# The low halves of the two gated branches computed on VectorE instead of GpSimd

## The chip, the cores and the metric

The kernel runs on one core of a Trainium2 chip. A core has five engines that run side by side, each with its own in-order instruction queue: TensorE (PE: matmuls, with PEld for its weight loads), VectorE (DVE), ScalarE (ACT), GpSimd (POOL) and SyncE (SP, which here only issues DMAs). They wait for one another through semaphores. The metric is device time in microseconds (us) of one execution, over several runs. A profile is one more execution under the hardware profiler.

## The reference

Two layers of a transformer trunk for 512 latent and 256 context tokens, model width 1024. Each layer has two parallel attention branches that share one input projection: A is a 2-D neighbourhood attention with 8 heads of 64 channels, B is a grouped-query attention with 8 query heads. Each branch is multiplied by its own gate, projected to the model width, weighted by a sigmoid gate, and the sum goes through one output projection:

```
def _merge(a_att, b_att, a_z, b_z, g_a, g_b, w_o_a, w_o_b, w_out):
    o_a = (a_att * jax.nn.silu(a_z)) @ w_o_a
    o_b = (b_att * jax.nn.silu(b_z)) @ w_o_b
    merged = jax.nn.sigmoid(g_a) * o_a + jax.nn.sigmoid(g_b) * o_b
    return merged @ w_out
```

The first factor of each product in front of `w_o_a` and `w_o_b` is what this document calls a gated branch. Layer 0 computes all 768 tokens, layer 1 only the 512 latent ones.

## The kernel before

Matmuls run in a reduced 32-bit format. To keep the accuracy, each operand is split into a high part (the value rounded to that format, a cast on ACT) and a low part (the value minus its high part, a subtraction), and a product is three matmuls: high by high, low by high, high by low. In the projections these are lines L433, L434 and L435 (`mm3`). For the first piece of branch B in layer 0 they are L458, L459 and L461, where the last is the one that reads the low part of the activations.

Weights are streamed from memory by SP into three rotating buffers (`raw`), cast on ACT to `whi` (L418 or L403) and subtracted to `wlo` (L420 or L406) on POOL or DVE in turn (`mix_lo`). The gated branches are split by `hilo`: for each of the four 128-channel groups f of a branch, ACT casts the whole token range (L656) and an engine that the caller chooses subtracts (L657). The names in the profile are `za` to `gah` and `gal` for branch A, and `zb` to `gbh` and `gbl` for branch B.

A layer goes through these stages: the input projections; the neighbourhood attention, head by head, in which the gate projections run as filling work for PE; the key, value and query projections of branch B; then the grouped-query attention, again head by head, with the rest of the gate projections and the whole of branch A's output projection (`o_chunks("a")`) as filling work; and last the merge, with branch B's output projection and `w_out`.

In the grouped-query stage each head has four tiles of 128 queries. Per tile PE makes the scores (L861, L862, into `pss`, of which there are two buffers), DVE takes the maximum and copies the scores (L1131), ACT takes the exponential (L1132) and casts (L802), DVE or POOL subtracts the low half (L803), and SP issues a transposing DMA (L804). The next tile's scores can be written when ACT has read the buffer. In layer 0 a context tile follows (L874, L876, L880). The values are L1148 and L1149. The row sums are inverted on DVE (L809), transposed on PE (L811) and multiplied into the gate on DVE (L812). A head ends with ACT L795, DVE L796 and a product L797 into `zb`.

`prepare` is the first piece of filling work of branch A's output projection: it splits all four groups of `za` and loads the sigmoid gates `tg` (L660, SP). Each piece of that projection has twelve matmuls into the only `psf` buffer, and DVE then multiplies the result into `tg` (L692), which frees the buffer. `early` runs before the values of the last head: it loads the other two `tg` and splits groups 0 to 2 of `zb`, which are complete by then. Group 3 is split at the start of the merge, on DVE in both kernels.

The order in which each engine runs its instructions is not that of the source. The tile framework places all engines' instructions with a planner that has its own model of their durations (`schedule_with_timeline_sim=True`), so that another engine for one instruction can move the others too. On the chip each engine then keeps that fixed order.

Of the kernel before, what the change touches and what calls it, by code (L numbers as in the profile page):

```python
# [50 lines left out]
def R(ap):  # L51
    return ap.bitcast(F32R)
# [18 lines left out]
def hybrid_kernel(es: ExitStack, tc, x, ctx, cvec, w_ada, w_ada0, small, gvec, w_in, w_o_a, w_o_b, w_out,  # L71
                  bias_int, bias_edge, rope, ident_d, out):
    nc = tc.nc
    V, S, G, T = nc.vector, nc.scalar, nc.gpsimd, nc.tensor
# [14 lines left out]
    def big(name):  # L89
        return bigp.tile([128, 3072], F32, tag="big", name=nm(name))  # L90
# [493 lines left out]
    def layer(l, hx, nxt, start):  # L584
# [62 lines left out]
        gated = {}  # L647

        def hilo_tiles(name):
            return [big(name + part).rearrange("p (f n) -> p f n", f=4) for part in "hl"]  # L650

        def hilo(src, dst, fs, lo_eng=G, parts=((0, ntok),)):
            sv = src.rearrange("p (f n) -> p f n", f=4)
            for n0, n1 in parts:
                for f in fs:
                    S.copy(R(dst[0][:, f, n0:n1]), sv[:, f, n0:n1])  # L656
                    lo_eng.tensor_tensor(R(dst[1][:, f, n0:n1]), sv[:, f, n0:n1], dst[0][:, f, n0:n1], ALU.subtract)  # L657

        def load_tg(c):
            nc.sync.dma_start(tg[c].rearrange("p (f n) -> p f n", f=4)[:, :, :ntok], gs[c][:, :, :ntok])  # L660

        def o_chunks(br, prepare, evac):

            src = (w_o_a if br == "a" else w_o_b)[l]
            act = lambda part, k: gated[br][part][:, k, :]
            res = []
            for i in range(4):
                st = {}

                def ld(i=i, st=st):  # L670
                    st["w"] = load_w2(src, 256 * i, 4, pool_lo if br == "b" and i == 0 else mix_lo)
                pieces = [lambda f=f, n0=n0, n1=n1, i=i, st=st:
                          chan_proj(st["w"], f, act, n0, n1, lambda f, a, b, ps: evac(2 * i + f, a, b, ps),
                                    3 if br == "b" and i == 0 and first else 0)
                          for f in range(2) for n0, n1 in spans]
                res.append((ld, ([prepare] if i == 0 and prepare else []) + pieces))
            return res

        def prepare():

            gated["a"] = hilo_tiles("ga")
            hilo(za, gated["a"], range(4))
            for c in (0, 2):
                tg[c] = big("tg")
                load_tg(c)
# [56 lines left out]
        za = big("za")  # L742
# [16 lines left out]
        if True:  # L759
# [329 lines left out]
            hp["lag"] = 2  # L1089
            qbv = big("qb").rearrange("p (j n) -> p j n", j=4)  # L1090
            fill = in_order(gates[n_na:] + o_chunks("a", prepare, evac_a))
            run(fill, 2)

# [15 lines left out]
            zb = big("zb")  # L1109
# [55 lines left out]
            def early():  # L1165

                for c in (1, 3):
                    tg[c] = big("tg")
                    load_tg(c)
                gated["b"] = hilo_tiles("gb")  # L1170
                hilo(zb, gated["b"], range(3))
            own = {"cb": vbig[:, 1152:2176].rearrange("p (v n) -> p v n", v=2),
                   "junk": vbig[:, 2176:2432].bitcast(BF16)}
            bg = gate_steps((1,), Parts(att["p"], own)) if first else []
            pipeline(fill, 8, gq_first, values_of(zb, gq_values, vs[:, 1:2]), early, bg)
            gq_es.close()

# [322 lines left out]
```

## Time and profile before

| | us |
|---|---|
| median of 3 runs | 1125.91 |
| lowest and highest | 1125.44 and 1126.06 |
| the profiled execution's own time | 1127.56 |
| its span, from first to last instruction | 1125.6 |
| PE busy | 1093.3 (97%) |
| DVE busy | 774.7 (69%) |
| ACT busy | 579.0 (51%) |
| POOL busy | 490.6 (44%) |

The profiled execution is 1.65 us above the median of the runs, and 1.96 us of it lie outside the span. All times of day below count from the start of the span. A busy PE is not PE at its peak: its clock is granted in steps, and at a lower clock the same matmuls are busy for longer.

### The profile page before, as it was taken

To read this page: it belongs to the slowest core of one execution; us is meant where nothing else is said; L and a number is where in the kernel's file an instruction comes from. 1 tells how busy PE (TensorE), PEld (TensorE's weight loads), DVE (VectorE), ACT (ScalarE), POOL (GpSimd) and SP (SyncE) were. 2 spreads that over 40 slices of the span, in tenths; PEclk is the share of its full clock that TensorE was granted. 3 is DMA by queue.
4 is the path that set the end of the run, shared out by engine and by line. 5 is a ranking of instruction groups with operands and counts; after the bars stand their busy time and mean duration, and the time that the engine had idled before them with its cause. 6 is when DMAs were issued, how large, how long until landed. Compare 5 with 4: busy or idle time off the path is not lost.

```text
span 1125.6 us, 16862 instructions
## 1 busy us (share of the span) xinstructions
PE 1093.3 (97%) x5826; PEld 905.3 (80%) x5826; DVE 774.7 (69%) x1492; ACT 579.0 (51%) x1154; POOL 490.6 (44%) x405
## 2 busy tenths in 40 slices
PE   8999999999999999979999999999999999999998
PEld 5688888888998877757788888888888987776677
DVE  4666788897466477776577785458878765677473
ACT  6453266665433576755330284326666446776431
POOL 1054254654247144454521545235554563563531
PEclk9999999999999999989999999999999999999999
DMA  9454322242351488869633532553333236989742
GB/s 373 143 172 140 114 63 66 73 136 89 93 168 38 123 201 185 185 172 269 173 108 125 183 129 72 142 174 92 100 107 116 59 105 172 188 224 239 197 145 80
DMA packets 192222, 161.29 MB, mean 143 GB/s; under 512 B 116364, under 2 KB 158088, under 8 KB 190472
## 3 DMA queue, kind: packets, MB, share of 16 engines
q1 hardware_dynamic: 184800, 145.82, 46.8%
q0 software_dynamic: 2368, 7.87, 2.1%
q10 hardware_dynamic: 4968, 6.53, 1.7%
q8 instruction: 46, 0.75, 0.3%
q14 instruction: 40, 0.33, 0.1%
HBM read 115.58 MB, written 17.32 MB: 118 GB/s over the span
## 4 chain that ended last, share of the span: by engine, by line
PE 38%; issue 4%; DVE 3%; DMA 3%; POOL 2%; ACT 1%; SPq 1%; POOLq 0%; ACTq 0%
PE psx L435 6%; PE psx L433 6%; PE psx L434 6%; PE psf L433 4%; PE psf L434 4%; PE psf L435 4%; PE pss L955 1%; PE pss L861 1%; POOL wlo L406 1%; PE pss L862 1%; PE pst L779 1%; PE pst L1148 1%; DMA raw<-in_w_o_a_dram 1%; PE pst L1149 1%; DMA raw<-in_w_in_dram 1%
## 5 line engine op out<-in xcount | busy, mean ns | idle before, releaser
L420 POOL TENSOR_TENSOR wlo<-raw,whi 128x512 fp32r<-128x512 f32 x70 | 97.9, 1405 | 106.1 <-ACT whi L418 70.4
L433 PE MATMUL psf<-hx,whi 128*128 128x512 f32 (+1 forms) x360 | 138.0, 383 | 3.2 <-ACT zt L614 2.4
L435 PE MATMUL psf<-hx,wlo 128*128 128x512 f32 (+1 forms) x360 | 135.8, 377 | 0.0
L434 PE MATMUL psf<-hx,whi 128*128 128x512 f32 (+1 forms) x360 | 135.1, 375 | 0.0
L433 PE MATMUL psx<-whi,hx 128*128 128x512 f32 (+1 forms) x328 | 120.8, 372 | 0.0
L434 PE MATMUL psx<-wlo,hx 128*128 128x512 f32 (+1 forms) x328 | 119.6, 366 | 0.0
L435 PE MATMUL psx<-whi,hx 128*128 128x512 f32 (+1 forms) x328 | 119.5, 365 | 0.0
L418 ACT CAST whi<-raw 128x512 fp32r<-128x512 f32 x136 | 82.3, 620 | 64.0 <-DMA raw<-in_w_in_dram 35.3
L406 POOL TENSOR_TENSOR wlo<-raw,whi 128x512 fp32r<-128x512 f32 x40 | 61.2, 1535 | 122.1 <-ACT whi L403 80.1
L803 POOL TENSOR_TENSOR h<-p,h 128x768 f16<-128x768 f32 (+1 forms) x40 | 65.7, 1644 | 96.4 <-ACT h L802 72.0
L403 ACT CAST whi<-raw 128x512 fp32r<-128x512 f32 x88 | 54.1, 623 | 99.2 <-PE psx L435 34.2
L420 DVE TENSOR_TENSOR wlo<-raw,whi 128x512 fp32r<-128x512 f32 x66 | 73.6, 1115 | 30.6 <-ACT whi L418 29.0
L504 POOL TENSOR_TENSOR ss<-ss,ehalf 128x8 f32<-128x8 f32 (+2 forms) x40 | 62.5, 1566 | 72.9 <-DVE ss L501 72.8
L433 PEld LDWEIGHTS psf<-hx,whi 128*128 128x128 f32 x360 | 67.9, 188 | 15.4 <-ACT zt L614 3.7
L435 PEld LDWEIGHTS psf<-hx,wlo 128*128 128x128 f32 x360 | 67.8, 188 | 11.6
L1131 DVE CUSTOM_DVE_ANT_0 p<-pss,vb 128x768 f32<-128x768 f32 x64 | 60.3, 953 | 23.6 <-PE pss L862 21.1
L434 PEld LDWEIGHTS psf<-hx,whi 128*128 128x128 f32 x360 | 67.9, 189 | 10.3
L1132 ACT ACTIVATE p<-pss,mx 128x768 f32<-128x768 f32 x64 | 57.6, 900 | 34.7 <-DVE mx L1131 33.7
L435 PEld LDWEIGHTS psx<-whi,hx 128*128 128x128 f32 x328 | 61.9, 189 | 10.0
L434 PEld LDWEIGHTS psx<-wlo,hx 128*128 128x128 f32 x328 | 62.0, 189 | 9.2
L433 PEld LDWEIGHTS psx<-whi,hx 128*128 128x128 f32 x328 | 61.8, 189 | 8.9
L435 PE MATMUL psx<-hx,wlo 128*128 128x256 f32 (+1 forms) x208 | 68.0, 327 | 0.0
(362 smaller groups left out, 3095.8 us busy)
## 6 DMA issues: line engine op xcount, KB each, us to landing
raw<-in_w_in_dram SPq DMA_DIRECT2D x168, 256.0 KB, 2.9
rawb<-in_w_ada_dram SPq DMA_DIRECT2D x48, 256.0 KB, 2.8
raw<-in_w_out_dram SPq DMA_DIRECT2D x32, 256.0 KB, 2.9
tg<-gs SPq DMA_DIRECT2D x4, 1536.0 KB, 6.8
rawx<-in_w_ada_dram SPq DMA_DIRECT2D x4, 1024.0 KB, 9.8
rawy<-in_w_ada_dram SPq DMA_DIRECT2D x4, 1024.0 KB, 9.5
gs<-zt ACTq DMA_DIRECT2D x16, 256.0 KB, 2.0
raw<-in_w_o_a_dram SPq DMA_DIRECT2D x16, 256.0 KB, 3.4
```

The lines of the kernel that those rows point to most:

```text
L403: S.copy(hi[:, :n], raw[:, :n])
L406: e.tensor_tensor(lo[:, :n], raw[:, :n], F(hi[:, :n]), ALU.subtract)
L418: S.copy(hi, raw)
L420: lo_eng(i).tensor_tensor(lo, raw, F(hi), ALU.subtract)
L433: T.matmul(ps, lhs[0], rhs[0], start=first, stop=False)
L434: T.matmul(ps, lhs[0], rhs[1], start=False, stop=False)
L435: T.matmul(ps, lhs[1], rhs[0], start=False, stop=last)
L504: G.tensor_tensor(ss, ss, ehalf[:, :n], ALU.pow)
L779: T.transpose(pt[:, c0:c0 + 128], src, ident)
L803: eng.tensor_tensor(h[:, 1], p[:, :n], h[:, 0], ALU.subtract)
L1131: V.tensor_tensor_reduce(p, pss, lift, -1.0, 3e38, ALU.add, ALU.min, mx[:, 0:1])
L1132: S.activation(p, pss, AF.Exp, bias=mx[:, 0:1], accum_out=r[:, i:i + 1])
```

## The change

The two calls of `hilo` that took GpSimd, its default, now pass VectorE: four subtractions (L657) for `gal` and three for `gbl` in each layer, of 128x768 elements in layer 0 and 128x512 in layer 1. What is computed is the same, and the casts (L656) stay on ACT.

```
         def prepare():
 
             gated["a"] = hilo_tiles("ga")
-            hilo(za, gated["a"], range(4))
+            hilo(za, gated["a"], range(4), V)
             for c in (0, 2):
                 tg[c] = big("tg")
                 load_tg(c)
...
                 gated["b"] = hilo_tiles("gb")
-                hilo(zb, gated["b"], range(3))
+                hilo(zb, gated["b"], range(3), V)
```

Since the planner places the instructions anew, the built order of the changed kernel differs from the point where `gal` is made in layer 0 on to the first part of layer 1, and in a few places later in layer 1. Up to the first `gal` the order of every engine is the same in both kernels.

More of the change, by code (lines that the diff above doesn't have):

```diff
@@ L681, in prepare @@
             gated["a"] = hilo_tiles("ga")
-            hilo(za, gated["a"], range(4))
+            hilo(za, gated["a"], range(4), V)
             for c in (0, 2):
@@ L1170, in early @@
                 gated["b"] = hilo_tiles("gb")
-                hilo(zb, gated["b"], range(3))
+                hilo(zb, gated["b"], range(3), V)
             own = {"cb": vbig[:, 1152:2176].rearrange("p (v n) -> p v n", v=2),
```

## Prediction

> **What bounds the kernel now.** I read the page's totals first, then busy time by stretch, PE's waits by who ended them, and the engines' instructions in order of time where PE stands still.
>
> ```profile
> span 1125.6 us, 16862 instructions
> PE 1093.3 (97%) x5826; PEld 905.3 (80%) x5826; DVE 774.7 (69%) x1492; ACT 579.0 (51%) x1154; POOL 490.6 (44%) x405
> ...
> 490.00:500.00 10.00, 4.13 (x15) 2.80 (x13) 9.94 (x5) 6.71 (x15) 9.91 (x7) 0.83 0.99 341
> 500.00:510.00 10.00, 7.85 (x29) 5.58 (x30) 6.46 (x11) 1.83 (x3) 3.49 (x3) 0.66 0.48 104
> ...
> 550.00:560.00 10.00, 9.70 (x57) 8.34 (x57) 6.70 (x7) 1.40 (x3) 8.82 (x7) 1.00 0.67 213
> ```
>
> PE is busy 97% of the span, so the kernel is bound by PE and all that a change can give is the remaining 32 us of gaps, plus time lost at a lowered clock. One place stands out: from 490 to 510 (columns: stretch, length, busy time of PE, PEld, DVE, ACT, POOL, then granted clock, DMA share, GB/s) PE works 11.98 of 20 us and the granted clock is 0.83 and 0.66. There the layer-0 `gal` is made.
>
> ```profile
> PE psv L811 <- DVE ho L796: 5.8, 1, 5.8
> ...
> PE psf L434 <- POOL gbl L657: 1.0, 1, 1.0
> PE psf L434 <- POOL gal L657: 0.6, 1, 0.6
> ```
>
> These are PE's waits that touch the change (total, times, longest). The longest of the kernel, 5.8 us, is for DVE's L796, not for L657 itself. The order of time shows why (columns: start, duration, engine, line):
>
> ```profile
> 487.45 1.66 POOL L803 TENSOR_TENSOR h<-p,h 128x768 f16<-128x768 f32 x1 [5.72 <-ACT h L802]
> 489.08 1.29 POOL L797 TENSOR_TENSOR zb<-zb,ho 64x512 f32<-64x512 f32 x1
> 490.32 1.27 POOL L420 TENSOR_TENSOR wlo<-raw,whi 128x512 fp32r<-128x512 f32 x1
> 491.54 7.15 POOL L657 TENSOR_TENSOR gal<-za,gah 128x768 fp32r<-128x768 f32 x4
> 498.63 1.29 POOL L420 TENSOR_TENSOR wlo<-raw,whi 128x512 fp32r<-128x512 f32 x1
> ...
> 490.42 0.96 DVE L1131 CUSTOM_DVE_ANT_0 p<-pss,vb 128x768 f32<-128x768 f32 x1
> ...
> 492.20 8.26 DVE L420 TENSOR_TENSOR wlo<-raw,whi 128x512 fp32r<-128x512 f32 x1
> 500.49 0.95 DVE L855 TENSOR_TENSOR qs<-qb,qs 64x768 fp32r<-64x768 f32 x1
> ...
> 501.67 0.42 DVE L796 TENSOR_TENSOR ho<-psv,ho 64x256 f32<-64x256 f32 x1
> ...
> 510.81 0.69 DVE L420 TENSOR_TENSOR wlo<-raw,whi 128x512 fp32r<-128x512 f32 x1 [1.94 <-ACT whi L418]
> ```
>
> An L420 on DVE takes 0.69 us at 510.81 and 8.26 us at 492.20. The long one ends at 500.46, 0.54 us after the last of POOL's five gapless instructions (498.63 + 1.29 = 499.92): DVE was kept from its operands while POOL ran `gal` and the next `wlo`. Behind it stood L855, L809, L796, on which PE's L811 waited, and all score passes.
>
> **The change, part by part.** POOL loses 14 instructions, in these groups (count, total us and mean ns):
>
> ```profile
> L657 POOL TENSOR_TENSOR gal<-za,gah 128x768 fp32r<-128x768 f32 x4 | 7.1, 1832 | 0.0
> L657 POOL TENSOR_TENSOR gbl<-zb,gbh 128x768 fp32r<-128x768 f32 x3 | 6.8, 2298 | 0.0
> L657 POOL TENSOR_TENSOR gal<-za,gah 128x512 fp32r<-128x512 f32 x4 | 5.6, 1452 | 0.5 <-ACT gah L656 0.5
> L657 POOL TENSOR_TENSOR gbl<-zb,gbh 128x512 fp32r<-128x512 f32 x3 | 3.8, 1281 | 0.0
> ...
> 485.17 0.96 DVE L803 TENSOR_TENSOR h<-p,h 128x768 f16<-128x768 f32 x1 [0.67 <-ACT h L802]
> ```
>
> POOL gives up 7.1 + 6.8 + 5.6 + 3.8 = 23.3 us. DVE gets seven of 128x768 at 0.96 us, the L803 of that size at 485.17, and seven of 128x512 at 0.69: 11.6 us, which lifts it from 774.7 to 786 us, 70% of the span. No DMA and no cast is added; the two `tg` loads and `prepare` keep their place.
>
> *Layer 0, branch A.* PE's rows there:
>
> ```profile
> 487.80 3.03 ACT L656 CAST gah<-za 128x768 fp32r<-128x768 f32 x4
> ...
> 491.90 0.39 ACT L614 ACTIVATE zt<-psf 128x256 f32<-128x256 f32 x1
> ...
> 492.33 0.49 PE L433 MATMUL psf<-gah,whi 128*128 128x512 f32 x1 [1.62 <-ACT zt L614]
> 493.42 0.80 PE L434 MATMUL psf<-gal,whi 128*128 128x512 f32 x1 [0.59 <-POOL gal L657]
> ...
> 502.15 0.69 PE L811 MATMUL psv<-ident,r 128*128 128x128 f32 x2 [5.80 <-DVE ho L796]
> ...
> 503.91 0.63 PE L434 MATMUL psf<-gal,whi 128*128 128x512 f32 x1
> 504.34 0.63 PE L435 MATMUL psf<-gah,wlo 128*128 128x512 f32 x1
> ...
> 505.95 0.90 ACT L1132 ACTIVATE p<-pss,mx 128x768 f32<-128x768 f32 x1 [9.12 <-DVE mx L1131]
> ...
> 512.77 0.50 PE L433 MATMUL psf<-gah,whi 128*128 128x512 f32 x1 [0.28 <-DVE tg L692]
> ...
> 541.47 0.40 PE L434 MATMUL psf<-gal,whi 128*128 128x512 f32 x1
> 541.71 0.40 PE L435 MATMUL psf<-gah,wlo 128*128 128x512 f32 x1
> ...
> 544.79 0.38 PE L1148 MATMUL pst<-ht,vb 128*128 128x512 f16 x1 [0.61 <-DMA ht<-h]
> ...
> 547.16 0.38 PE L1149 MATMUL pst<-ht,vb 128*128 128x512 f16 x1
> ```
>
> A 128x512 matmul follows the one before it after 0.24 us at full clock (541.47 to 541.71) and after 0.43 us in the slow stretch (503.91 to 504.34); half the columns take half. The twelve passes of a head's values start 0.22 us apart (544.79 to 547.16). I walk through the changed kernel's built order with these durations, with 0.7 and 0.45 us for 512- and 256-wide operations on DVE that have no row of their own here. Until 492.33 nothing can differ for PE: it waits for ACT's L614 as now. Casts of `gah` finish from 488.6 to 490.83. DVE's queue reads: `gal` 0, L874, `gal` 1 and 2, L876, L812, `gal` 3, L420, L1131, L855, L796, L809, L692, L1131, L803, L812, L692. POOL's run L803, L797, L420 (487.45 to 491.59) still contends; with one POOL instruction let past ahead of each of the first three `gal` they end at about 490.1, 492.3 and 494.5, `gal` 3 after L812 at 496.6, L420 at 497.3 and the first score pass L1131 at 498.2 (490.42 + 0.96 = 491.4 now). So this tile's softmax is 6.8 us *later* than now; that is the cost of the edit here. PE runs all twelve matmuls of the first `w_o_a` piece ahead of the second tile's scores and ends them at 497.3, just behind `gal` 3. Scores of tile 2: 498.0 (two of 512 and two of 256 columns, 0.7 us). Tile 3 needs the buffer of tile 1, released by its exponential (0.90) at 499.2, and ends at 499.9; L811 at 500.3 (L855, L796 and 0.2 us of L809 after 498.2). The second piece waits for L692 (0.7) to free `psf`: 500.5 to 501.9. Tile 4 waits for the exponential of tile 2 at 502.4, and ends at 503.1. The third piece waits for L692 behind an L803 and an L812, 503.3 to 506.1. Values take 2.6 us, the context values 0.6 (four half-width passes and their start) and the context scores 0.5: 509.8.
>
> In the trace of before the third piece starts at 512.77 and so ends at 512.77 + 12 x 0.23 = 515.5, with the same work behind it except the context values of 0.6 us: 516.1. **Gain 6.3 us**, if PE's clock is full. If it is low until 506.5 as now, each of the passages above that isn't waiting for DVE stretches by 0.43/0.23 and the walk ends 2.1 us later: gain 4.2 us. I take the middle, 5.2.
>
> The rule in the Trainium skill that bears on this speaks against the change: "SBUF — State Buffer", section "Who interferes with whom", has a VectorE instruction with two SBUF inputs and a GpSimd instruction that reads SBUF exclude each other, the later one waiting until the earlier one finishes. By it the moved subtractions meet the lock-out themselves, as the walk counts with rows of its own. The trace agrees with one instruction's wait at 550.79, quoted below, but at 492.20 the wait spanned five; by the page the lock-out alone would not explain that row, and the sum would be that of the second rival.
>
> *Layer 0, branch B.*
>
> ```profile
> 550.79 2.23 DVE L420 TENSOR_TENSOR wlo<-raw,whi 128x512 fp32r<-128x512 f32 x1
> ...
> 1002.62 1.44 DVE L420 TENSOR_TENSOR wlo<-raw,whi 128x512 fp32r<-128x512 f32 x1
> ...
> 1052.24 0.50 PE L434 MATMUL psf<-gbl,whi 128*128 128x512 f32 x1 [1.05 <-POOL gbl L657]
> ...
> 1081.17 7.74 POOL L406 TENSOR_TENSOR wlo<-raw,whi 128x512 fp32r<-128x512 f32 x2 [4.81 <-ACT whi L403]
> ```
>
> Here the POOL run of `gbl` holds DVE for only one instruction (2.23 us). Moved, three times 0.96 us stand in DVE's queue ahead of an L692 that frees `psf`; PE's built order has the b-branch's high parts to do meanwhile, and needs `gbl` 2 some 0.5 us after it gets there. PE waits about that long there now for L692 and the rest: I take 0. Without that cover the price is 3 x 0.96 = 2.9 us, and the most to be gained is the 0.3 us that PE idles from 550 to 560 in today's order; bounds -0.3 to +2.9.
>
> *Layer 1.* `gal` as four 0.69 us on DVE falls where DVE waits for scores; L420 was held 1.44 us there and is freed. Cost at most 4 x 0.69 = 2.8 us if the softmax waits behind it, none if DVE's idle time takes it. At `gbl` PE waits 1.05 us for POOL (1052.24), and DVE can have `gbl` 0 earlier by about that. I take -0.5 for both, bounds -1.05 to +2.8.
>
> **Sum:** -5.2 + 0 - 0.5 = -5.7 us. The profiled execution's 1127.56 becomes 1121.9, and the median 1125.91 of the runs, 1.65 below it, becomes 1120.2.
>
> **The rivals.**
>
> *All of it is regained.* PE's 5.8 and 0.6 us go, L657's 1.0 us goes, and the clock never drops: from 493.4 to 496.3 and from 502.2 to 506.9, 7.6 us at 0.43 instead of 0.23 per matmul, 3.5 us. In all 10.9: 1115.0. Against it stands DVE's queue, in which the score passes are now late.
>
> *The wait was not POOL's doing* or comes back behind other POOL work in the same place. Then the 8.26 us stay, and of the 0.6 and 1.0 us some half goes by estimate: 1125. For it speaks that DVE got in between POOL's `gbl` instructions at 550.79 and between `gal` at 1002.62; against it that the long L420 ends 0.54 us after POOL's run does, about the 0.69 it needs alone.
>
> *Slower: the lock-out moves with the work.* A subtraction on DVE is shut out by a POOL run in the new order, as L420 was at 492.20, or POOL by a DVE run, as in 1081.17, where two L406 took 7.74 us. One such lock-out of 8.26 - 0.69 = 7.6 us on PE's path with the clock loss of 3.5 behind it costs 11.1 against 5.7 gained: 1131.3. The likeliest place is the layer-0 head stage after 490. It decides from a lock-out of 4.5 us on (5.7 + 2.3 - 3.5). The trace has one of this length on PE's path in two dense layers.
>
> **How the numbers follow.** Forecast 0.54, all regained 0.17, not the cause 0.13, lock-out moved 0.16. Runs tell about 0.2%, 2.25 us, from no change. The forecast's own range is 1118.3 to 1124.6: 7.65 us gained if the clock is full and both small terms stand at their best, 1.3 if the clock is low and layer 0's branch B costs its 2.9. Faster by over 0.2% are the first two, less 0.03 for the forecast's upper edge: 0.68; within 0.2% the third and that edge: 0.16; slower: 0.16. The range from 1114, 1 us below the best case, to 1127, 1 us above the median now, leaves out the slower case and little of the rest.
>
> **What would show it.** Right: no DVE L420 above 3 us near 492, PE's wait for L796 at L811 gone or below 1 us, L657 on DVE near 0.96 and 0.69 us plus at most one POOL instruction, PE busy 15 or more of the 20 us from 490 to 510. Wrong: a new wait of PE above 4 us, on `gal`, `gbl`, `psf` or L1132, or a clock below 0.9 over more than these 20 us.

## The result, and the profile after

The changed kernel takes 1130.2 us (median of 6 runs, 1128.72 to 1131.08), the kernel before, in runs beside it, 1125.99 (6 runs, 1122.63 to 1128.07). The ratio is 1.0030 with a 95% interval of 1.0018 to 1.0042: slower by 0.3%, and outside the range of the prediction. The profiled execution of the changed kernel took 1128.72 us, at the fast end of its runs, so the profile shows the smaller part of the difference: 1128.72 against 1127.56.

The totals of its page:

```profile
span 1126.9 us, 16859 instructions
PE 1090.9 (97%) x5826; PEld 903.5 (80%) x5826; DVE 776.8 (69%) x1506; ACT 580.5 (52%) x1154; POOL 468.9 (42%) x391
```

PE does the same 5826 matmuls and is busy 2.4 us less than before (1093.3). Some 1.8 us of that come from fewer matmuls at a lowered clock: busy time times the share of the clock that is missing, summed over 490 to 510, falls from 3.4 to 1.6 us. POOL has given up 21.7 us, DVE has taken on 2.1. By the prediction's durations DVE has 11.6 us of new work, so on balance it is shut out for some 9.5 us less than before.

Busy time by stretch, kernel before first and then the changed one (stretch, length, busy time of PE, PEld, DVE, ACT, POOL, granted clock, DMA share, GB/s):

```profile
510.00:560.00 50.00, 47.30 (x265) 37.01 (x264) 29.54 (x50) 23.83 (x46) 25.67 (x19) 1.00 0.80 209
650.00:670.00 20.00, 20.00 (x102) 16.59 (x101) 18.54 (x26) 18.71 (x48) 12.29 (x14) 1.00 0.37 123
```

```profile
490.00:500.00 10.00, 5.30 (x24) 3.56 (x23) 9.84 (x12) 6.43 (x15) 5.88 (x4) 0.98 1.00 335
500.00:510.00 10.00, 10.00 (x49) 7.59 (x50) 6.85 (x15) 4.91 (x9) 2.40 (x2) 0.85 0.88 233
510.00:560.00 50.00, 44.15 (x256) 35.63 (x254) 32.70 (x56) 23.57 (x46) 18.90 (x16) 1.00 0.88 223
650.00:670.00 20.00, 17.26 (x82) 12.90 (x81) 17.81 (x29) 16.89 (x41) 10.71 (x11) 1.00 0.34 106
```

Busy time times granted clock is the work that PE got done. From 490 to 510 that is 5.30 x 0.98 + 10 x 0.85 = 13.7 us against 4.13 x 0.83 + 7.85 x 0.66 = 8.6 before: 5.1 us gained, where the prediction had 5.2. From 510 to 560 it is 44.15 against 47.30: 3.2 lost. From 560 to 640 PE is busy throughout in both kernels. From 650 to 670 it is 17.3 against 20.0: 2.7 lost. So within the first layer the whole gain is given back, in two stretches for which the prediction's sum had 0 or no term.

The wait of 5.8 us for L796 at L811 is gone. These waits of PE have grown or are new (total, times, longest); the first came to 2.3 us in the kernel before, the second to 0.3, the other two were not there:

```profile
PE pst L1148 <- DMA ht<-h: 4.6, 4, 1.5
PE psx L458 <- DVE ho L796: 1.7, 1, 1.7
PE pst L341 <- ACT half L344: 1.3, 2, 1.0
PE psx L434 <- DVE wlo L406: 1.0, 1, 1.0
```

The place of the old lock-out, in order of time, DVE, then POOL, then PE:

```profile
488.71 1.27 DVE L657 TENSOR_TENSOR gal<-za,gah 128x768 fp32r<-128x768 f32 x1 [1.30 <-PE psf L435]
490.50 1.43 DVE L657 TENSOR_TENSOR gal<-za,gah 128x768 fp32r<-128x768 f32 x1
491.85 3.28 DVE L657 TENSOR_TENSOR gal<-za,gah 128x768 fp32r<-128x768 f32 x1
496.03 0.96 DVE L657 TENSOR_TENSOR gal<-za,gah 128x768 fp32r<-128x768 f32 x1
496.90 0.68 DVE L420 TENSOR_TENSOR wlo<-raw,whi 128x512 fp32r<-128x512 f32 x1
497.62 0.96 DVE L1131 CUSTOM_DVE_ANT_0 p<-pss,vb 128x768 f32<-128x768 f32 x1
...
489.13 1.98 POOL L797 TENSOR_TENSOR zb<-zb,ho 64x512 f32<-64x512 f32 x1
491.08 3.23 POOL L420 TENSOR_TENSOR wlo<-raw,whi 128x512 fp32r<-128x512 f32 x2
...
495.19 0.50 PE L434 MATMUL psf<-gal,whi 128*128 128x512 f32 x1 [0.92 <-DVE gal L657]
497.05 0.50 PE L434 MATMUL psf<-gal,whi 128*128 128x512 f32 x1 [0.90 <-DVE gal L657]
499.73 0.79 PE L861 MATMUL pss<-gk,qs 128*128 128x512 f32 x1 [1.25 <-ACT p L1132]
501.17 0.63 PE L811 MATMUL psv<-ident,r 128*128 128x128 f32 x2
```

L420 on DVE takes 0.68 us in the place where it took 8.26. Two of the four `gal` take 1.43 and 3.28 us instead of 0.96 each. The first ends at 491.93, 0.82 us after POOL's L797 (489.13 + 1.98 = 491.11). The next ends at 495.13, 0.82 us after the second of POOL's two L420 (491.08 + 3.23 = 494.31), although only the first of them was running when it started. PE waits for them twice (0.92, 0.90) and once for ACT's exponential (1.25), and the 5.80 us at L811 are gone.

The first place where the gain goes is the end of the heads: four pieces of `gbl` ahead of the L796 that frees `psv`, for which PE's L458 waits. The kernel before, then the changed one (DVE, then PE):

```profile
553.05 0.43 DVE L796 TENSOR_TENSOR ho<-psv,ho 64x256 f32<-64x256 f32 x1
...
553.54 0.50 PE L458 MATMUL psx<-gbh,whi 128*128 128x512 f32 x1 [0.30 <-DVE ho L796]
```

```profile
543.19 4.36 DVE L657 TENSOR_TENSOR gbl<-zb,gbh 128x768 fp32r<-128x768 f32 x4
545.80 1.75 DVE L657 TENSOR_TENSOR gbl<-zb,gbh 128x512 fp32r<-128x512 f32 x1
547.58 0.43 DVE L796 TENSOR_TENSOR ho<-psv,ho 64x256 f32<-64x256 f32 x1
...
537.05 0.38 PE L1148 MATMUL pst<-ht,vb 128*128 128x512 f16 x1 [1.53 <-DMA ht<-h]
548.07 0.50 PE L458 MATMUL psx<-gbh,whi 128*128 128x512 f32 x1 [1.75 <-DVE ho L796]
```

The second row is the last of the four pieces by itself: it belongs to group 3, which VectorE makes in both kernels. In the kernel before it comes behind that L796; here the planner has put it ahead as well, and it takes 1.75 of the 4.36 us, beside an L420 of POOL.

The second place is the boundary of the layers. To see it one needs a part of the kernel that the change doesn't touch. Layer 1's modulation `modc` comes from a product with `w_ada`, spread over the `w_out` stage of layer 0 as work for DVE: 16 tiles of 256 KB go through two buffers `rawb`, loaded on POOL's DMA queue (L288), with two dot products on DVE each (L295); a short chain then makes `modc` (last instruction L240), which ACT needs for the first input of layer 1 (L344, behind PE's L341). The finished rows of layer 0 leave as stores of 512 KB, on POOL's queue too (L1229):

```
            cb["w"] = pool.tile([128, 512], F32, tag="rawb", name=nm("rawb"), bufs=2)
            (queue or nc.sync).dma_start(cb["w"], w_ada[l, h, i])
...
                            G.dma_start(xs1[128 * t:128 * t + 128, :], xt)
```

In the kernel before all 16 loads are issued ahead of the first store. In the changed kernel the planner's order has two stores ahead of the last two loads. The kernel before, then the changed one, in order of time (POOL's queue, DVE, PE):

```profile
642.32 0.55 POOL L288 DMA_DIRECT2D rawb<-in_w_ada_dram  x1 [2.31 <-DVE asum L295]
642.92 0.55 POOL L1229 DMA_DIRECT2D xs<-xt  x1
...
649.75 0.17 DVE L240 TENSOR_TENSOR modc<-modc,g 128x16 f32<-128x16 f32 x1
```

```profile
639.53 0.55 POOL L1229 DMA_DIRECT2D xs<-xt  x1
642.05 0.63 POOL L1229 DMA_DIRECT2D xs<-xt  x1
642.68 0.97 POOL L288 DMA_DIRECT2D rawb<-in_w_ada_dram  x1
645.03 1.09 POOL L288 DMA_DIRECT2D rawb<-in_w_ada_dram  x1 [0.47 <-DVE asum L295]
...
647.77 0.69 DVE L295 CUSTOM_DVE_ANT_0 junk<-rawb,cb 128x512 bf16<-128x512 f32 x1 [1.77 <-DMA rawb<-in_w_ada_dram]
652.72 0.18 DVE L240 TENSOR_TENSOR modc<-modc,g 128x16 f32<-128x16 f32 x1
...
655.01 0.66 PE L341 MATMUL pst<-ident,y 128*128 128x128 f32 x4 [0.99 <-ACT half L344]
```

The last such load on the chain that ended last, in either kernel, again before and after (start, duration, what):

```profile
642.32 3.14 DMA rawb<-in_w_ada_dram
```

```profile
642.68 5.06 DMA rawb<-in_w_ada_dram
```

Behind a store the load takes 5.06 us instead of 3.14, DVE stands still for it (1.77), and `modc` is complete at 652.9 instead of 649.9, though the rest of the stage runs ahead of the kernel before. Of PE's 2.7 us, 1.3 are waits for L344, which needs `modc`; 1.2 are waits at L434 for low parts of weights (L406). The longer of these, 1.01, ends with an L406 on DVE at 660.34, the last of a run without a gap that DVE could begin only at 654.99, after standing 2.08 us for L344.

The Trainium skill ("DMA: Bandwidth & Descriptors", section "Queues, rings and completion order") gives each queue a ring of its own on every DMA engine, and has an engine go round between the queues that have work for it. The rows fit a load that starts behind a store on its own ring, and so does the run below in which the stores leave that queue: there the last load lands in 2.88 us. The distance to the store matters: the late load here, and that of the run with only `gbl` of layer 0 moved, were issued 0.63 us after one; in the run with only `gal` of layer 0, a load issued 1.17 us after a store landed in 3.2 us.

### The profile page after: what moved, and what is told of

The parts are those of the page before. It is cut to its first block, busy times and chain, and to the rows that moved or that the text cites. A ratio compares the mean times of both kernels' runs of the same rounds, so it can differ in the third digit from the quotient of the medians.

```text
span 1126.9 us, 16859 instructions
## 1 busy us (share of the span) xinstructions
PE 1090.9 (97%) x5826; PEld 903.5 (80%) x5826; DVE 776.8 (69%) x1506; ACT 580.5 (52%) x1154; POOL 468.9 (42%) x391
## 4 chain that ended last, share of the span: by engine, by line
PE 72%; DVE 9%; issue 7%; DMA 5%; ACT 4%; POOL 3%; SPq 0%; ACTq 0%; POOLq 0%; DVEq 0%
PE psx L435 9%; PE psx L434 9%; PE psx L433 9%; PE psf L433 8%; PE psf L434 8%; PE psf L435 8%; PE pst L779 2%; DMA ht<-h 2%; PE pss L955 2%; PE pss L861 2%; PE pss L862 2%; PE pst L525 1%; PE pst L1148 1%; PE pst L1149 1%; DMA rawb<-in_w_ada_dram 1%
## 5 line engine op out<-in xcount | busy, mean ns | idle before, releaser
L420 POOL TENSOR_TENSOR wlo<-raw,whi 128x512 fp32r<-128x512 f32 x70 | 99.9, 1435 | 120.7 <-ACT whi L418 68.1
L434 PE MATMUL psf<-hx,whi 128*128 128x512 f32 (+1 forms) x360 | 135.1, 375 | 0.0
L434 PE MATMUL psx<-wlo,hx 128*128 128x512 f32 (+1 forms) x328 | 120.3, 367 | 1.2 <-DVE wlo L406 1.0
L406 POOL TENSOR_TENSOR wlo<-raw,whi 128x512 fp32r<-128x512 f32 x40 | 59.8, 1498 | 128.2 <-ACT whi L403 86.9
L420 DVE TENSOR_TENSOR wlo<-raw,whi 128x512 fp32r<-128x512 f32 x66 | 64.9, 983 | 28.3 <-ACT whi L418 26.7
L433 PEld LDWEIGHTS psf<-hx,whi 128*128 128x128 f32 x360 | 67.9, 188 | 15.3 <-ACT zt L614 3.6
L435 PEld LDWEIGHTS psf<-hx,wlo 128*128 128x128 f32 x360 | 67.8, 188 | 11.6
L434 PEld LDWEIGHTS psf<-hx,whi 128*128 128x128 f32 x360 | 67.9, 189 | 10.4
L434 PEld LDWEIGHTS psx<-wlo,hx 128*128 128x128 f32 x328 | 62.0, 189 | 11.1 <-DVE wlo L406 1.4
```

The costliest lines, as they stand in the source:

```text
L406: e.tensor_tensor(lo[:, :n], raw[:, :n], F(hi[:, :n]), ALU.subtract)
L420: lo_eng(i).tensor_tensor(lo, raw, F(hi), ALU.subtract)
L433: T.matmul(ps, lhs[0], rhs[0], start=first, stop=False)
L434: T.matmul(ps, lhs[0], rhs[1], start=False, stop=False)
L435: T.matmul(ps, lhs[1], rhs[0], start=False, stop=last)
```

## Experiments

Each group of runs was made on one chip, with the kernel before beside it. In the table, work is PE's busy time times granted clock in stretches of some 4 us, counted from the matmul that starts at 492.33 in the kernel before, so that a kernel that comes there earlier or later is compared at the same work; each figure is the difference to the kernel before. The first column is built from the same instructions in all kernels with `gal` on VectorE and still reads from 5.6 to 6.8, so 1 us of it is the granted clock: after the same four waits of PE (1.63, 0.92, 0.90 and 1.26 us) it fell to about 0.6 (0.57 to 0.66) over some 4 us in the four profiled executions that read +5.6, and stayed at 1.00 in those that read +6.8.

| kernel | 492 to 510 | 510 to 560 | 640 to 680 | median | ratio (95%) |
|---|---|---|---|---|---|
| the change | +5.6 | -3.2 | -2.7 | 1130.2 | 1.0030 (1.0018 to 1.0042) |
| gal of layer 0 | +5.6 | -1.0 | -1.8 | 1126.9 | 0.9991 (0.9981 to 1.0001) |
| gbl of layer 0 | +0.5 | -0.3 | -3.4 | 1132.7 | 1.0042 (1.0029 to 1.0055) |
| the change, third buffer | +6.8 | -4.1 | -0.4 | 1126.1 | 0.9993 (0.9982 to 1.0003) |
| gal of layer 0, third buffer | +5.6 | -1.8 | -0.4 | 1124.1 | 0.9974 (0.9963 to 0.9984) |
| gbl of layer 0, third buffer | 0.0 | -0.2 | +0.1 | 1127.3 | 1.0012 (1.0004 to 1.0021) |
| layer 0, third buffer | +6.8 | -2.6 | -0.4 | 1125.2 | 0.9991 (0.9982 to 0.9999) |
| layer 0, third buffer, gbl late | +6.8 | -0.7 | -0.5 | 1122.4 | 0.9967 (0.9955 to 0.9979) |
| layer 0, gbl late | +5.6 | -1.0 | -3.0 | 1128.4 | 1.0014 (1.0005 to 1.0023) |

### Each of the four parts alone

```
-            hilo(za, gated["a"], range(4), V)
+            hilo(za, gated["a"], range(4), V if first else G)
...
-                hilo(zb, gated["b"], range(3), V)
+                hilo(zb, gated["b"], range(3), G)
```

and likewise for the other three, with GpSimd (`G`) wherever the part isn't the one named.

> Only the gal of layer 0 is made on VectorE; its gbl and both of layer 1 stay on GpSimd. Theory (a gain at 490 to 510 us that the rest of layer 0 doesn't keep, because the end of layer 0 is set by the layer-1 adaLN chain and by the order of the work behind 510): the wait of L811 for L796 is gone, PE is 5 to 6 us ahead at 510 to 585, and the time is between 1 us less and 3 us more than before. Rival 1 (gal gains as predicted, the loss is gbl's or layer 1's): 1120 to 1122. Rival 2 (gal on VectorE is itself the loss): 1129 to 1131, as the whole change.

> Only the gbl of layer 0 is made on VectorE. Theory: the wait of 5.8 us at L811 stays and nothing is gained there; 510 to 600 gets dearer by up to 3 us, of which some may be lost in the end of layer 0: 1126 to 1129. Rival 1 (gbl carries the loss of the whole change and the gain of gal hides part of it): 1129 to 1134. Rival 2 (gal is itself the loss): 1126, no change.

> Only the gal of layer 1 is made on VectorE. Prediction on record: 0 to -0.5 us with bounds -1.05 to +2.8 for both parts of layer 1. Theory that layer 1 matters little: 1125.5 to 1127. Rival, that layer 1 carries the loss: 1128 or more, with the softmax of the heads around it late.

> Only the gbl of layer 1 is made on VectorE. Theory: the wait of 1.05 us for the low part becomes 0.7: 1125 to 1126.5. Rival, that layer 1 carries the loss: 1128 or more.

Measured: `gal` of layer 0 1126.88 (0.9991), `gbl` of layer 0 1132.66 (1.0042), `gal` of layer 1 1128.53 (1.0015, 1.0006 to 1.0025), `gbl` of layer 1 1126.86 (1.0000, 0.9991 to 1.0009). The part that was costed at nothing, `gbl` of layer 0, costs 4.7 us (0.42% of 1127): the first rival of the second run. The table says where: only 0.3 us of PE's work is lost near it, 3.4 us are lost 100 us later. The chain that ended last in that kernel has the late load again:

```profile
646.64 5.19 DMA rawb<-in_w_ada_dram
```

Its POOL queue has two stores ahead of the last load only, so one late load is enough. `gal` of layer 0 does bring its 5.6 us, but 2.8 of them are lost behind it. `gal` of layer 1 came out in its rival's range, 1.7 us slower. That is not explained by one wait; from 1000 to 1060 PE did 0.6 us less than before.

### A third buffer for the late loads

```
-            cb["w"] = pool.tile([128, 512], F32, tag="rawb", name=nm("rawb"), bufs=2)
+            cb["w"] = pool.tile([128, 512], F32, tag="rawb", name=nm("rawb"), bufs=3 if queue else 2)
```

With it all 16 loads stand ahead of the first store, in every kernel.

> The changed kernel with a third buffer for the w_ada tiles of the layer-1 adaLN (L287), so that GpSimd's queue issues all 16 loads ahead of the first store of a finished row tile (L1229). Theory (the gain of layer 0 is lost at 650 to 670 us, because the last two loads come behind these stores and the modulation is ready at 652.7 instead of 649.8): the modulation is ready by 649, PE loses less than 1 us from 650 to 670 instead of 2.7, and the time is 1124.5 to 1127.5. Rival (the loss is in the order of the work from 510 to 550 alone, or in the moved subtractions): 1129 to 1131, as the change without the third buffer.

> The kernel before with the same third buffer, as a control. Theory: its 16 loads are all ahead of the stores already and the modulation is in time (PE waits for nothing from 650 to 660), so nothing changes: 1125 to 1127. Rival (the third buffer speeds up either kernel): 1122 to 1124.

> Only the gal of layer 0 on VectorE, with the third buffer. Theory: what the gal gains in the head stage (PE some 4 us ahead at 585) reaches the end: 1122 to 1124.5, less than either kernel. Rival (the lead is absorbed at the layer boundary by something else than the loads, such as the weight splits): 1126 to 1127.5, as without the third buffer.

> Only the gbl of layer 0 on VectorE, with the third buffer for the w_ada tiles. Theory (of the 4.7 us that this part cost alone, some 3.5 are the late modulation at 650 to 670, the rest is PE's longer wait for the last heads' L796 behind the gbl): PE loses under 1 us from 650 to 680 instead of 3.5, time 1126.5 to 1128.5. Rival (the moved gbl itself costs it): 1130.5 or more.

Measured: the change 1126.12 (from 1.0030 to 0.9993), the kernel before 1126.11 (0.9995, 0.9986 to 1.0004), `gal` alone 1124.12 (from 0.9991 to 0.9974), `gbl` alone 1127.34 (from 1.0042 to 1.0012). Busy time by stretch of the changed kernel with three buffers, where it had 17.26:

```profile
650.00:670.00 20.00, 19.55 (x98) 15.52 (x97) 14.58 (x21) 15.48 (x40) 8.51 (x10) 1.00 0.33 107
```

So the buffer is worth 0.37 and 0.30% to the two kernels whose loads were late behind stores, and nothing to the kernel before, in which no load stands behind one. The layer boundary is thus shown to be where 3 to 4 us of the change went: in the table the boundary recovers 2.3 us, while the two stretches ahead of it change from +2.4 to +2.7 together. The buffer is also worth 0.17% to `gal` alone, and there the reason is not a late load: its one load behind stores landed in 3.2 us, `modc` was complete at 645.7, and PE's waits at the boundary were 1.3 us for low parts of weights (L406) and 0.6 for L344. What the buffer changes there is not shown. `gal` alone with it is faster than either kernel, by 0.26%.

### The stores on another queue

```
-                            G.dma_start(xs1[128 * t:128 * t + 128, :], xt)
+                            nc.sync.dma_start(xs1[128 * t:128 * t + 128, :], xt)
```

> The changed kernel with the four stores of L1229 issued on SyncE's queue instead of GpSimd's; two buffers as before. Theory, as for the third buffer but by the other end (the loads no longer stand behind stores in their queue; a store on SyncE can hold weight loads up instead): the modulation is ready by 650.5, 1125 to 1128.5. Rival (late for want of a free buffer, not for the stores): no change, 1129 to 1131.

Measured: 1129.62 (1.0024, 1.0012 to 1.0035), outside the theory's range and inside the rival's. The profiled execution, 1126.58, was the fastest of these runs. The loads were indeed freed: the last one is issued at 644.37, DVE's product with it starts at 647.27, and `modc` is complete at 650.4. But SyncE's queue issues the weights of layer 1, and stands still behind the stores, which wait for their rows (SyncE, then PE):

```profile
642.60 7.53 SPq L1229 DMA_DIRECT2D xs<-xt  x2
...
658.71 0.50 PE L434 MATMUL psx<-wlo,hx 128*128 128x512 f32 x1 [1.29 <-POOL wlo L406]
```

PE lost 2.6 us from 640 to 680, nearly as before, now 2.0 of them to low parts of weights that come late. The rival's reason does not hold, since with two buffers `modc` came within the 650.5 that the theory named. But the run doesn't confirm the theory's gain either: the loads came early, and the wait moved to another queue.

### What layer 1 and gbl cost beside that

> Both parts of layer 0 on VectorE, layer 1 as before, third buffer. Against the whole change with the third buffer (1126.1) it shows what layer 1 costs, against gal alone with it (1124.1) what the gbl of layer 0 costs. Theory: gbl costs 1.5 (the wait at L458 of 1.75 instead of 0.25), the rest of the 2.0 is layer 1: 1125 to 1126. Rivals: all of it is layer 1, 1124; all of it is gbl, 1126.1 or more.

Measured: 1125.2 (0.9991). Against `gal` alone with the third buffer (0.9974) the `gbl` of layer 0 costs 0.17%, 1.9 us; against the whole change with it (0.9993) layer 1 costs 0.02%, nothing that can be measured. Both are near what the theory had; the intervals of the first pair (0.9982 to 0.9999 and 0.9963 to 0.9984) just overlap. The 1.7 us of `gal` in layer 1 alone thus do not show beside the other edits, and stay unexplained.

### Fewer of the four gal

```
-            hilo(za, gated["a"], range(4), V)
+            [hilo(za, gated["a"], [f], V if first and f < 2 else G) for f in range(4)]
```

and with `f < 3`; third buffer and all else on GpSimd.

> Only gal 0 and 1 of layer 0 on VectorE, 2 and 3 and all else on GpSimd, third buffer. Theory (the gain is the end of the gapless GpSimd run that shut VectorE out for 8.26 us; two gal less are enough to open it, and GpSimd's two cost VectorE no more than one instruction each): L811 waits less than 1.5 us for L796, and the time is 1122.5 to 1125. Rival (with GpSimd still at gal the lock-out comes back): the wait of over 4 us stays, 1126.

> gal 0 to 2 of layer 0 on VectorE, gal 3 and all else on GpSimd, third buffer. Theory: as all four of gal with the third buffer or a little less, 1122.5 to 1125, since VectorE is spared 0.96 us ahead of the first score pass. Rival: the planner's order around it decides, and it comes out over 1125.5.

Measured: two of four 1127.08 (0.9998, 0.9987 to 1.0010), three 1125.27 (0.9984, 0.9974 to 0.9994), four 1124.12 (0.9974). The first run is about as slow as its rival said, and the lock-out comes back, with two `gal` left on POOL, on an instruction of two columns; but PE's wait of over 4 us does not: it waits 1.95 us at L811 and 1.90 at L861. The second lies between the ranges of theory and rival. The lock-out (DVE, POOL):

```profile
491.52 4.81 DVE L876 TENSOR_SCALAR mx<-mx 128x2 f32<-128x2 f32 x1
...
490.74 1.98 POOL L420 TENSOR_TENSOR wlo<-raw,whi 128x512 fp32r<-128x512 f32 x1
492.69 3.60 POOL L657 TENSOR_TENSOR gal<-za,gah 128x768 fp32r<-128x768 f32 x2
```

L876 reads and writes 128x2 elements and took 4.81 us, to the end of POOL's two `gal`; in the changed kernel it takes 0.16 us (at 495.05). It waited out the L420 that was running and both `gal`; the expectation that a DVE instruction waits for one POOL instruction only was wrong here.

### The last head: casts, and the place of gbl

Two edits, each with the third buffer. The first pins ScalarE's casts of `gbh` in program order, the second puts `gbl` 0 to 2 behind the last head's values and pins them there:

```
-                hilo(zb, gated["b"], range(3), G)
+                behind(ON_ACT, lambda: hilo(zb, gated["b"], range(3), G))
```

```
-                hilo(zb, gated["b"], range(3), V if first else G)
...
             pipeline(fill, 8, gq_first, values_of(zb, gq_values, vs[:, 1:2]), early, bg)
+            behind(ON_DVE, lambda: hilo(zb, gated["b"], range(3), V if first else G))
```

> As gal alone with the third buffer (1124.1), and ScalarE's three casts of gbh (L656, 2.3 us) pinned in program order, which puts the last score tile's cast of h (L802) ahead of them. Theory (the lead of 6 us at 510 shrinks because PE runs out of fill and waits 1.7 us at L1148 for the last head's transposed h, whose cast stands behind these casts): the wait at L1148 falls below 0.5 us and the time to 1122.5 to 1123.8. Rival (the last head is held by its scores or by the transpose queue): the wait stays over 1 us, 1124 to 1125.

> Control: the kernel before with the third buffer and the same pinned casts. Its wait at L1148 is 0.6 us, so at most that much goes: 1125.5 to 1126.5. Rival (the pinned casts help or hurt either kernel alike): the same difference as gal alone shows.

> Both parts of layer 0 on VectorE with the third buffer (1125.2), and gbl 0 to 2 kept behind the last head's L796 on VectorE. Theory (gbl costs 1 to 2 us because it stands ahead of that L796, whose psv PE's L458 waits for, 1.75 instead of 0.25 us): that wait falls below 0.6 us and the time to 1123.5 to 1124.7. Rival (the price of gbl is that PE gets its low parts later or VectorE is busy): a wait of over 1 us on gbl or psf in its place, 1125 to 1126.

The pinned casts: 1125.26 (0.9987, 0.9976 to 0.9997) against 0.9974 without the pin; the kernel before 1127.83 (1.0012, 1.0003 to 1.0021). PE's wait at L1148 did go from 1.72 us to nothing, and another came in its place (PE):

```profile
530.10 0.50 PE L433 MATMUL psf<-gah,whi 128*128 128x512 f32 x1 [1.93 <-DVE tg L692]
```

In the kernel without the pin that wait was 0.51, and by the table's measure the stretch from 510 to 560 reads -2.0 with it and -1.8 without. So the theory on the casts falls as a way to keep the lead: the end of the heads is a chain of several links, and PE, once ahead, runs out of other work and waits for whichever is last. The time itself says little on this, because the pin holds in layer 1 too: from 1000 to 1060 PE did 4.2 us less with it than in the kernel before, and 1.7 us less in the control, whose time lies above its range. What is left of `gal`'s loss from 510 to 560, 1 to 2 us, stays open beyond this.

The late `gbl`: 1122.36 us, ratio 0.9967 (0.9955 to 0.9979), the fastest of all and below the range expected. L796 now comes ahead of the subtractions, and no wait of PE at L458 is left (DVE; below it busy time by stretch, where the change had 44.15):

```profile
542.92 0.43 DVE L796 TENSOR_TENSOR ho<-psv,ho 64x256 f32<-64x256 f32 x1
543.38 4.35 DVE L657 TENSOR_TENSOR gbl<-zb,gbh 128x768 fp32r<-128x768 f32 x3
```

```profile
510.00:560.00 50.00, 46.57 (x276) 38.24 (x275) 34.19 (x60) 24.00 (x47) 19.94 (x17) 1.00 0.89 235
```

The subtractions still take VectorE 4.35 us, so it was the place of `gbl` in its queue, ahead of one L796 of 0.43 us, and not the engine that made it, which cost 1.9 us and more.

### The controls of that version

> The whole change, both layers, with the third buffer and gbl 0 to 2 kept behind the last head's L796 in both layers. Theory (layer 1 is worth nothing either way): as layer 0 alone with the same two edits, 1122 to 1123.5. Rival (gal of layer 1 costs 1.7, as it did alone): 1123.5 to 1125.

> Control: low parts on GpSimd as before, with the third buffer and the same statement order for gbl. Theory: gbl wasn't ahead of any L796 on VectorE here, nothing changes, 1125.5 to 1127. Rival (the new order gives the gain by itself, whoever makes the low parts): 1122 to 1124.

> Both parts of layer 0 on VectorE and gbl 0 to 2 kept behind the last L796, but two buffers for the w_ada tiles as before, so that two loads again stand behind stores on GpSimd's queue. Theory (the layer boundary takes what the head stage gained): PE loses 2 us or more from 650 to 670, 1125.5 to 1127.5. Rival (with gbl in its new place the boundary no longer matters): 1122 to 1123.5.

The kernel before with both edits: 1126.96 (1.0001, 0.9990 to 1.0011), so the gain is not that of the edits alone. Without the third buffer: 1128.42 (1.0014), slower than the theory's range, with 3.0 us lost from 640 to 680; the third buffer thus decides between 0.9967 and 1.0014, 5.3 us, of which the two profiles show 2.5 at the boundary and some 1 us in the clock.

```profile
650.00:670.00 20.00, 17.02 (x81) 12.68 (x80) 17.79 (x33) 15.96 (x39) 9.89 (x11) 1.00 0.33 107
```

With layer 1 treated alike: 1130.51 (1.0040, 1.0028 to 1.0053), far off either expectation. There the pinned order harms: PE waits 4.40 us for the last head's transposed `h` and 2.90 us for a `gbl` that now comes last, at a lowered clock (PE; below it busy time by stretch):

```profile
1050.26 0.61 PE L1148 MATMUL pst<-ht,vb 128*128 128x512 f16 x1 [4.40 <-DMA ht<-h]
1058.19 0.71 PE L434 MATMUL psf<-gbl,whi 128*128 128x512 f32 x1 [2.90 <-DVE gbl L657]
```

```profile
1050.00:1060.00 10.00, 6.84 (x17) 3.08 (x18) 3.88 (x6) 1.20 (x2) 0.00 (x0) 0.67 0.45 154
```

In layer 0 the b-branch has its high parts to do while it waits for `gbl`; in layer 1 every product takes its low part in turn (L434). This run says nothing on what layer 1 costs; the comparison above does.

## Why the prediction was wrong

*Layer 0, branch A, at its place: right.* Forecast 5.2 us gained by about 510, between 4.2 at a low clock and 6.3 at a full one; measured 5.1 in the stretch, and +5.6 and +6.8 by the table's measure in runs with a lowered and a full clock. The walk held: the first score pass was to end at 498.2 and ended at 498.58, L811 was to start at 500.3 and started at 501.17. That the middle of the two clocks was hit within 0.1 us is luck. One detail was off: one POOL instruction was let past ahead of each `gal`. For `gal` 1 that was right (491.93, forecast 492.3), but `gal` 2 waited out two and ended at 495.13 instead of 494.5. The Trainium skill ("SBUF — State Buffer", section "Who interferes with whom") has a VectorE instruction with two SBUF inputs and a GpSimd instruction that reads SBUF contend for a port that is held for a whole instruction. The trace agrees for `gal` 1, which waited for one instruction of POOL; `gal` 2 waited for two, and the L420 that took 8.26 us before for five, which this does not explain.

*Layer 0, branch A, from there to the end: wrong.* The step that failed is the comparison at 516, "with the same work behind it": the gain was carried from there to the end of the kernel as if PE alone set the pace and all else kept its order. Runs show two places where that fails. The last head is one that PE reaches early only to wait (1 to 2 us). The layer boundary comes later by itself: `modc` is complete 3.0 us later than before, which costs 2.7 us in the profile and 3.4 to 4.2 by the runs with and without the third buffer, and it costs `gbl` alone 3.4 us, where there is no lead to lose. The prediction noted that no DMA is added, which is true, and put no price on their order, although the built order was known to differ up to the first part of layer 1. The sum had no term for either place, and no bound.

*Layer 0, branch B: mis-sized.* It was costed at 0 with bounds of -0.3 to +2.9, with the high parts of the b-branch as cover. The cover was there for `gbl` itself, but what PE waited for was the L796 queued behind it, 1.75 us at L458; measured 1.9 us, inside the bounds. By the rows above, the piece of group 3 that the planner put ahead as well decides it, as an estimate: without its 1.75 us L796 would have ended at 546.26, and PE came to L458 at 546.32. With `gbl` alone and the third buffer, where L796 stands ahead of that piece, the wait is 0.68. The larger part of its price alone, 3.4 us of 4.7, was the order of loads and stores on POOL's DMA queue, on which the forecast had no sentence although the layer boundary's transfers are issued by the engine that lost the work.

*Layer 1:* forecast -0.5, measured +0.02% with the third buffer (0.2 us), inside the bounds. At `gbl` PE waits 0.72 for DVE instead of 1.05 for POOL.

```profile
1053.32 0.50 PE L434 MATMUL psx<-gbl,whi 128*128 128x512 f32 x1 [0.72 <-DVE gbl L657]
```

*The range.* Its upper end, 1124.6, took branch B at its worst, 2.9 us, but not layer 1 at its 2.8. With both the loss would be 1.5 us, 1127.4; the measured 1130.2 lies beyond that too, so a term was missing and not only mis-sized.

*The rivals.* "Not POOL's doing" falls with the 0.68 us of L420, and "all of it is regained" with PE's waits of 0.92, 0.90 and 1.25 us and the clock of 0.85 in the same place. The slower rival named nearly the right time, 1131.3, for the wrong reason: no lock-out above 4.5 us is on PE's path. The signs of being right that the prediction named all came, but for a `gal` held longer than one POOL instruction, and no sign of being wrong: PE busy 15.3 of 20 us, no new wait above 4 us, clock below 0.9 only from 500 to 510. They looked at one place and at single waits; the loss came as waits of 0.99 to 1.75 us, 40 and 150 us later.

*What stays open.* The profiled executions put the change 1.2 us behind the kernel before, the medians 3.4 to 4.2; no view of them shows the rest. Nor is it shown why freeing the loads on another queue gained nothing in time, or what the third buffer gives `gal` alone. Runs of one kernel scatter by 2 to 7 us, so single waits below 1 us are read here, not proven.

## What to carry to other kernels

A local gain is worth what survives to the next place at which the engine must wait for something that the edit did not speed up; before summing, follow the lead to each such place (the last head's chain, the transfers that open the next layer) and ask what would release the engine there. Where a planner orders all queues, compare the DMA order of the engine whose work was moved with that of before, above all loads that stand right behind stores, since two such loads here took back 2.7 of the 5.1 us gained. A count of the DMAs does not show it. An instruction moved to a faster engine still belongs behind the one that someone is waiting for: 0.43 us of L796 behind 4.4 us of `gbl` cost 1.9 us.

## What the runs showed of the hardware

A VectorE instruction on 128x2 elements was shut out for 4.81 us while POOL ran three subtractions without a gap. Of two 128x768 subtractions on VectorE, one ended 0.82 us after the one POOL instruction that was running when it started, the next 0.82 us after a second one. The kernel before has the reverse at 1081.17: a 128x512 subtraction on POOL took 6.49 us beside a run of VectorE without a gap.

A 256 KB load issued 0.63 us after a 512 KB store on POOL's queue took 5.06 and 5.19 us; one issued 1.17 us after took 3.2, and one with no store ahead 3.14.

TensorE's granted clock fell to 0.83 over the ten microseconds from 530 after one wait of 1.93 us (the pinned casts), and to 0.67 from 1050 after 4.40 us (both layers late). After 1.75 us at 548.07 in the changed kernel it stayed at 1.00. The same four waits within 9 us, from 490 on, lowered it in four profiled executions and not in four others, so the length of the waits alone does not decide.
